# A two-layer decoder trunk on one core: the last up-projection chunk of each feed-forward block also by seven products

## The chip, the cores and the metric

One core of a Trainium2 chip. The time is device microseconds of one launch; lower is better. TensorE (PE) multiplies 128x128 tiles, its weight loads (PEld) run beside it; VectorE (DVE), ScalarE (ACT) and GpSimd (POOL) do elementwise work; SyncE (SP) and POOL issue DMAs. Each engine has its own instruction stream and runs it strictly in order; semaphores tie the streams together.

## The reference

`x` is 512 tokens by 1024. There are two layers, each an attention mixer and then a gated feed-forward block, with root-mean-square norms before and after each. The change touches only the feed-forward block, which both layers have:

```
def conv_ffn(xn, w_up, cw, cb, w_down):          # xn 512x1024, w_up 1024x5632, w_down 2816x1024
    a = xn @ w_up
    a = sum(ap[:, j:j + T] * cw[j] for j in range(3)) + cb      # causal, depthwise over tokens
    gate, val = jnp.split(a, 2, axis=-1)
    return (jax.nn.gelu(gate, approximate=True) * val) @ w_down
```

Everything is float32.

## The kernel before

**Three matmuls for one.** A float32 operand is split into a high part, which a cast to the matmul type gives, and a low part, the rest. Each product is `ah*bh + ah*bl + al*bh` (`mm3`, lines 292 to 294), into one PSUM bank. So every weight needs a cast on ACT (high) and a subtraction on DVE (low). In some places the low part is made another way: ACT writes the negative of the raw weight (`scale=-1.0`) rounded to the matmul type, and an adding DMA from POOL's queue adds the raw weight to it in SBUF.

**Chunks.** The up-projection's 2 x 2816 columns are done in 22 chunks `c` of 128 gate and 128 value columns, features on partitions and the 512 tokens in the free dimension. A plain chunk is two banks (gate and value) of 8 steps over the contraction, 3 matmuls each, 512 wide: 48 matmuls. A chunk in `SEVEN` uses Winograd's form of Strassen's algorithm over halves of the tokens and the contraction and the two column groups: seven products of 12 matmuls, 256 wide (84), some of them accumulated onto each other in PSUM. Its operands are sums of the four weight blocks A11, A12, A21, A22 (`S1` to `S4`, made in `seven_weights`), and sums of the inputs (`XA`, `XB`). The four quarters `o1` to `o4` of its two banks are finished with copies on ACT (`s1`, `u2`, `s7`) and three additions on DVE. `open_seven` does the first product of the next chunk ahead of the last product (`S4`) of the current one. Before, chunks 3 to 20 are so done and 0, 1, 2 and 21 are plain.

**After the matmuls** come, for each of the two banks: the middle tap of the convolution with the bias on ACT (`first_tap`), the two other taps on DVE (`other_taps`, two instructions), then the GELU on ACT (`glu`) and the product of gate and value on POOL (`product`), which a DMA stores in DRAM (`hD`).

**Down-projection.** `down` works on 11 pairs `j` of chunks, again with seven products. In its first part `mul_one(j, bp)` does four of them (12 matmuls, 512 wide) for each token block `bp`, in the order (0,0), (1,0), (0,1), (1,1), (2,0), (2,1), (3,0) and so on; pair 0 opens all eight PSUM banks, four for each `bp`. A pair needs three operands, called `wa`, `wb` (weights) and `ac` (activations): two raw weight tiles (loaded by SP; some sums of w_down lie ready in DRAM as `dT`) and the activations `dact` (from `hD`), whose three sums `pair_sums` makes on DVE. `pair_highs` casts the three on ACT, `pair_lows` subtracts on DVE. In `mul_one` the first of the four products uses `wa`, the second and third `wb`, the fourth `wa`; the low part of the weight is read by the second matmul of each product, the low part of `ac` by the third.

**Order.** It is written out by hand (`manual_schedule`): each engine does its instructions in the order in which the program gives them. The loop over `c` has generators (`step`) that put pieces of the next chunks' weight work between the current chunk's. Below, c is the chunk, m = c + 1 and n = c + 2.

Of the kernel before, what the change touches and what calls it, by code (L numbers as in the profile page):

```python
# [108 lines left out]
def trunk_kernel(ctx, tc, x, norm_gains, w_qkv_a, w_o_a, w_q_b, w_o_b, kv_norm, w_kvf, b_f,  # L109
# [581 lines left out]
    def ffn(l, bd, cp, nxt, ahead):  # L691
# [4 lines left out]
        def first_tap(bb, i, ps, ch):  # L696
            act.activation(bb[:, i, :], ps, AF.Identity, bias=cp[:, 3, ch:ch + 1], scale=cp[:, 2, ch:ch + 1])  # L697

        def other_taps(bb, i, ps, ch):
            for n in (1, 2):  # L700
                dve.scalar_tensor_tensor(bb[:, i, n:], ps[:, :T - n], cp[:, 2 - n, ch:ch + 1], bb[:, i, n:],  # L701
                                         ALU.mult, ALU.add)

        def taps(c, banks, between=None):
            bb = t4([128, 2, T], name="bb")
            for i, ch in ((0, c), (1, NF + c)):
                first_tap(bb, i, banks[i], ch)
                other_taps(bb, i, banks[i], ch)
                if i == 0 and between is not None:
                    between()  # L710
            return bb

        gated = []

        def product():

            if gated:
                c, bb = gated.pop()
                hc[c] = t2([128, T], name="hc")
                pool.tensor_tensor(hc[c], bb[:, 0, :], bb[:, 1, :], ALU.mult)  # L720
                if c - 1 in hc:
                    pool.dma_start(hD[c - 1], hc.pop(c - 1))

# [1 line left out]
            act.activation(bb[:, 0, :], bb[:, 0, :], AF.Gelu_apprx_tanh)  # L725
            gated.append((c, bb))

        def post(c, banks, between=None, bb=None):
            product()
            if bb is None:  # L730
                bb = taps(c, banks, between)
            else:
                first_tap(bb, 0, banks[0], c)
                other_taps(bb, 0, banks[0], c)
                if between is not None:
                    between()
            glu(c, bb)

        xT = None
        XA, XB = [], []  # L740
# [51 lines left out]
            yield  # L792
            dve.tensor_tensor(v[:, 1], r0, v[:, 0].bitcast(F32), ALU.subtract)

        def plain_weights(c):
            W.high_added()
            yield
            W.high()
            yield
            W.low()  # L800

        gens = {}

        def step(c, n=1):

            if c >= NF or c < 0:
                return
            if c not in gens:
                gens[c] = (seven_weights if c in SEVEN else plain_weights)(c)
# [5 lines left out]
        a11, s1_, s3_, s2_ = (slice(i * 256, i * 256 + 256) for i in range(4))  # L815

        def pair_load(j):

# [14 lines left out]
        def pair_highs(j):  # L833

            raws[j] = [*W.take(2), acts.pop(j)]
            one[j] = [t8([128, 2, 1024], F32R, name="w") for _ in range(3)]
            for w, r in zip(one[j], raws[j]):
                act.copy(w[:, 0], r)

        def pair_lows(j):  # L840
            parts = [*zip(one[j], raws.pop(j))]
            for w, r in (parts[0], parts[2], parts[1]) if j == 2 else (parts[2], parts[0], parts[1]):
                dve.tensor_tensor(w[:, 1], r, w[:, 0].bitcast(F32), ALU.subtract)  # L843

        def load_two(j):

# [61 lines left out]
            p_11(j, bp)  # L908
            p_12(j, bp)

        def run(steps):
            for _ in steps:
                pass

        def down(nxt, ahead):
            pair_highs(3)
            for bp in range(2):
                for j in range(2):
                    mul_one(j, bp)
            for j in range(1, ND - 2):  # L920
                if j > 1:
                    mul_one(j, 0)
                    mul_one(j, 1)
                if j + 3 < ND:
                    pair_sums(j + 3)
                    pair_lows(j + 2)
                    pair_highs(j + 3)
                elif j + 3 == ND:
                    pair_lows(j + 2)
                    load_two(0)  # L930
            pair_two(0)
            pair_two(1)
# [76 lines left out]
        step(S0, 2)  # L1009
        post(0, first[0:2])  # L1010
        step(S0, 2)
        begun = opened = half_taps = None
        kept = []
        beside = sums_beside(kept, (l, ND - 1), (1, 8 + l))
        before = 1, first[2:4]
# [11 lines left out]
        for c in range(2, NF):  # L1027
            if c == NF - 4:
                pair_load(0)
            m, n = c + 1, c + 2  # L1030
            if c in SEVEN:
                x21, x22 = [(xT[0][i], xT[1][i], s) for i, s in ((1, LO), (1, HI))]
                banks, s1 = opened
                opened = None
                w = halves.pop(c)
                W.n_get += 2
                o1, o2, o3, o4 = banks[0][:, LO], banks[0][:, HI], banks[1][:, LO], banks[1][:, HI]
                u2, s7 = (t2([128, 256], name="csum") for _ in range(2))
# [3 lines left out]
                bb = half_taps or t4([128, 2, T], name="bb")  # L1042
                cb, prev = before
                for i, ch in ((1, NF + cb), (0, cb)):
                    if i == 0 or half_taps is None:
                        first_tap(bb, i, prev[i], ch)
                        other_taps(bb, i, prev[i], ch)
                half_taps = None
                if n in SEVEN:
                    step(n)  # L1050
                act.copy(u2, o2)
                step(n, 1 if n in SEVEN else 2)
# [4 lines left out]
                if m in SEVEN:  # L1057
                    step(m, 2)
                if n in SEVEN:
                    step(n)  # L1060
                next(beside, None)
                dve.tensor_tensor(o1, o1, s1, ALU.add)
                if m in SEVEN:
                    step(m)
                prod(o3, w.pop("A22"), (*XB, LO))
                dve.tensor_tensor(o4, o2, s7, ALU.add)
                dve.tensor_tensor(o3, o3, u2, ALU.add)
                if n in SEVEN:
                    step(n)
                half_taps = t4([128, 2, T], name="bb")  # L1070
                first_tap(half_taps, 1, banks[1], NF + c)
                if m in SEVEN:
                    opened = open_seven(m)
                    step(m)
                else:
                    begun = W.get(), bank([128, T], name="up")
                    up(*begun, range(4))
                    XA.clear()
                    XB.clear()
                    step(m)  # L1080
                    pair_highs(0)
                    pair_sums(1)
                other_taps(half_taps, 1, banks[1], NF + c)
                while kept:
                    sp.dma_start(*kept.pop())
                prod(o2, w.pop("S4"), x22)
            else:
                banks = [bank([128, T], name="up") for _ in range(2)]
                for s in range(2):
                    if s == 0 and begun:  # L1090
                        w, banks[0] = begun
                        up(*begun, range(4, KD))
                        begun = None
                    else:
                        up(W.get(), banks[1 - s if m in SEVEN else s], range(KD))
                    if s == 0 and m in SEVEN:
                        opened = open_seven(m)
                    if s == 0:
                        post(*before, (lambda: pair_lows(0)) if c == NF - 1 else None, half_taps)
                        half_taps = None  # L1100
                        if c == NF - 1:
                            pair_highs(1)
                    if n not in SEVEN:
                        step(n, 2 - s)
                    if s == 0 and m in SEVEN:
                        half_taps = t4([128, 2, T], name="bb")
                        first_tap(half_taps, 1, banks[1], NF + c)
                        other_taps(half_taps, 1, banks[1], NF + c)
            before = c, banks
            if c == NF - 3:  # L1110
                pair_sums(0)
# [916 lines left out]
```

## Time and profile before

| | us |
|---|---|
| median of 3 runs (1091.5 to 1092.33) | 1092.04 |
| the profiled execution, its own time | 1092.08 |
| span in its profile, first to last instruction | 1090.3 |
| PE busy | 1081.9 (99%) |
| DVE / ACT / POOL busy | 908.7 / 750.9 / 304.5 |
| first feed-forward block: first matmul of chunk 20 after its opening product | 385.64 |
| first feed-forward block: first matmul of the down-projection | 405.21 |
| the same two in the second block | 959.78, 979.35 |

The profile's page lists busy time by engine, the span in 40 slices, DMA queues, the chain of work that ended last, and the costliest groups. In the timeline a row is a start, a duration, the engine, the line, what is written and read, and in brackets the idle time before it with what ended that. PE's rows overlap, since matmuls are pipelined: what a matmul costs is the distance from one start to the next.

### The profile page before, as it was taken

The numbers are of one execution on the slowest core, as the hardware profiler recorded it, in microseconds if no ns is written. First come the engines' busy times: TensorE is split into PE (matmuls) and PEld (weight loads), VectorE is DVE, ScalarE is ACT, GpSimd is POOL, SyncE is SP. The second block draws the span as 40 slices with busy tenths as digits, with TensorE's granted clock in tenths as the row PEclk, the third lists the DMA queues.
The fourth block names the chain that finished last, engine by engine and source line by source line (L and its number), as shares of the span: only waits on it lengthen the run. The fifth ranks groups of instructions, "written<-read, shape, count | busy, mean of one in ns | idle before, by whom it ended". The sixth has DMA issues, their size and how long they took to land.

```text
span 1090.3 us, 20004 instructions
## 1 busy us (share of the span) xinstructions
PE 1081.9 (99%) x7184; PEld 964.7 (88%) x7184; DVE 908.7 (83%) x1510; ACT 750.9 (69%) x1290; POOL 304.5 (28%) x405
## 2 busy tenths in 40 slices
PE   9999999999999999999999999999999999999997
PEld 6988889999999998888888788789999999998886
DVE  6677768898999889997877877937898998989995
ACT  6654587778788757576565677766787878756573
POOL 4632110333333322000010667610233333322000
PEclk9999999999999999999999999999999999999999
DMA  9679895689999978894872776597689999978972
GB/s 314 137 275 407 339 238 156 145 204 233 248 227 223 258 230 319 326 319 106 213 155 78 215 228 196 159 291 185 131 206 240 241 226 239 239 228 315 343 261 77
DMA packets 198251, 250.03 MB, mean 229 GB/s; under 512 B 13888, under 2 KB 141880, under 8 KB 197640
## 3 DMA queue, kind: packets, MB, share of 16 engines
q1 hardware_dynamic: 175976, 181.86, 52.0%
q0 software_dynamic: 22176, 66.90, 28.5%
q8 instruction: 56, 0.92, 0.3%
q14 instruction: 43, 0.35, 0.1%
HBM read 170.28 MB, written 39.63 MB: 193 GB/s over the span
## 4 chain that ended last, share of the span: by engine, by line
PE 91%; DVE 4%; ACT 2%; issue 1%; DMA 0%; SPq 0%; DVEq 0%; ACTq 0%
PE up L292 12%; PE up L293 12%; PE up L294 12%; PE acc L293 7%; PE acc L292 7%; PE acc L294 7%; DVE w L843 2%; PE v_ps L292 2%; PE v_ps L293 2%; PE v_ps L294 2%; PE qk_ps L1361 2%; PE o_ps L1880 2%; PE s_ps L1833 2%; PE q_ps L292 2%; PE pT_ps L1865 2%; PE first L294 1%
## 5 line engine op out<-in xcount | busy, mean ns | idle before, releaser
L292 PE MATMUL up<-xsh,w 128*128 128x256 f32 x576 | 163.1, 283 | 0.0
L293 PE MATMUL up<-xsl,w 128*128 128x256 f32 x576 | 163.0, 283 | 0.0
L294 PE MATMUL up<-xsh,w 128*128 128x256 f32 x576 | 163.0, 283 | 0.0
L701 DVE SCALAR_TENSOR_TENSOR bb<-up,conv,bb 128x511 f32<-128x511 f32 (+1 forms) x160 | 119.4, 747 | 11.7 <-ACT bb L697 8.9
L292 PE MATMUL acc<-w 128*128 128x512 f32 (+1 forms) x311 | 120.6, 388 | 0.0
L294 PE MATMUL acc<-w 128*128 128x512 f32 (+1 forms) x311 | 120.4, 387 | 0.0
L293 PEld LDWEIGHTS up<-xsl,w 128*128 128x128 f32 x576 | 110.6, 192 | 0.1
L292 PEld LDWEIGHTS up<-xsh,w 128*128 128x128 f32 x576 | 110.6, 192 | 0.1
L294 PEld LDWEIGHTS up<-xsh,w 128*128 128x128 f32 x576 | 110.6, 192 | 0.0
L293 PE MATMUL acc<-w 128*128 128x512 f32 (+1 forms) x267 | 103.5, 388 | 0.1
L697 ACT ACTIVATE bb<-up,conv 128x512 f32<-128x512 f32 x80 | 62.3, 779 | 44.3 <-PE up L294 34.2
L770 POOL DMA_DIRECT2D w<-wraw x36 | 30.8, 857 | 164.2 <-ACT w L769 146.5
L720 POOL TENSOR_TENSOR hc<-bb 128x512 f32<-128x512 f32 x44 | 68.4, 1555 | 22.8 <-ACT bb L725 14.5
L60 ACT CAST w<-wraw 128x1024 fp32r<-128x1024 f32 x64 | 66.5, 1051 | 8.1 <-issue 3.8
L294 PEld LDWEIGHTS acc<-w 128*128 128x128 f32 x311 | 58.4, 188 | 11.9
L292 PEld LDWEIGHTS acc<-w 128*128 128x128 f32 x311 | 58.4, 188 | 11.9
L69 DVE TENSOR_TENSOR w<-wraw,w 128x1024 fp32r<-128x1024 f32 x44 | 54.3, 1249 | 10.6 <-ACT w L60 10.5
L293 PEld LDWEIGHTS acc<-w 128*128 128x128 f32 x267 | 50.1, 188 | 11.0 <-DVE w L843 0.9
L781 ACT CAST w<-wsum 128x1024 fp32r<-128x1024 f32 x36 | 37.9, 1052 | 30.2 <-DVE wsum L778 30.2
L843 DVE TENSOR_TENSOR w<-wraw,w 128x1024 fp32r<-128x1024 f32 x44 | 54.1, 1266 | 0.0
L293 PE MATMUL up<-xbl,w 128*128 128x256 f32 (+1 forms) x176 | 53.2, 303 | 0.0
L293 PE MATMUL up<-xcl,w 128*128 128x256 f32 (+1 forms) x176 | 53.2, 303 | 0.0
(348 smaller groups left out, 3482.3 us busy)
## 6 DMA issues: line engine op xcount, KB each, us to landing
wraw<-in_w_up_dram SPq DMA_DIRECT2D x144, 256.0 KB
w<-wraw POOLq DMA_DIRECT2D x56, 512.0 KB, 6.3
dT<-dsums SPq DMA_DIRECT2D x34, 512.0 KB
hD<-hc POOLq DMA_DIRECT2D x44, 256.0 KB, 6.2
dact<-hD SPq DMA_DIRECT2D x44, 256.0 KB
wraw<-dT SPq DMA_DIRECT2D x22, 512.0 KB
wraw<-in_w_down_dram SPq DMA_DIRECT2D x22, 512.0 KB
dsums<-in_w_down_dram SPq DMA_DIRECT2D x36, 256.0 KB
```

What stands on the lines that cost most here:

```text
L60: self.nc.scalar.copy(pair[:, 0, s], raw[:, s])
L69: self.nc.vector.tensor_tensor(pair[:, 1, s], raw[:, s], pair[:, 0, s].bitcast(F32), ALU.subtract)
L292: pe.matmul(o, ah, bh, start=first, stop=False, skip_group_check=shared)
L293: pe.matmul(o, ah, bl, start=False, stop=False, skip_group_check=shared)
L294: pe.matmul(o, al, bh, start=False, stop=last, skip_group_check=shared)
L697: act.activation(bb[:, i, :], ps, AF.Identity, bias=cp[:, 3, ch:ch + 1], scale=cp[:, 2, ch:ch + 1])
L701: dve.scalar_tensor_tensor(bb[:, i, n:], ps[:, :T - n], cp[:, 2 - n, ch:ch + 1], bb[:, i, n:], ALU.mult, ALU.add)
L720: pool.tensor_tensor(hc[c], bb[:, 0, :], bb[:, 1, :], ALU.mult)
L770: pool.dma_start(b[:, 1], r1, accum_op=ALU.add)
L781: act.copy(u[:, 0], sb)
L843: dve.tensor_tensor(w[:, 1], r, w[:, 0].bitcast(F32), ALU.subtract)
L1361: pe.matmul(o, ax(0, b, kc)[x], w[:, k, :], start=kc == 0 and x == 0 and w is wh, stop=kc == KD - 1 and w is wl)
```

## The change

`SEVEN` goes from chunks 3..20 to chunks 3..21, so chunk 21 is done by seven products too, in each of the two feed-forward blocks. The plain way for chunk 21 (`plain_weights`, `begun`, the branches on `n in SEVEN`) goes away. Chunk 21 gets a tail of its own, with the first weight work of the down-projection between its products:

```
@@ SEVEN
-SEVEN = tuple(range(3, 21))
+SEVEN = tuple(range(3, 22))
@@ pair_highs, and a new function behind it
-            for w, r in zip(one[j], raws[j]):
+            parts = [*zip(one[j], raws[j])]
+            for w, r in (parts[2], parts[0], parts[1]) if j < 2 else parts:
                 act.copy(w[:, 0], r)
+                if j == 0:
+                    yield
+
+        def pair_third():
+            j = 2
+            raw = W.take(2)
+            one[j] = wa, wb, ac = [t8([128, 2, 1024], F32R, name="w") for _ in range(3)]
+            act.copy(wa[:, 0], raw[0])
+            act.copy(wb[:, 0], raw[1])
+            act.activation(wb[:, 1], raw[1], AF.Copy, scale=-1.0)
+            pool.dma_start(wb[:, 1], raw[1], accum_op=ALU.add)
+            yield
+            pair_sums(j)
+            k = acts.pop(j)
+            act.copy(ac[:, 0], k)
+            for w, r in ((wa, raw[0]), (ac, k)):
+                dve.tensor_tensor(w[:, 1], r, w[:, 0].bitcast(F32), ALU.subtract)
@@ the loop over chunks, behind the first two products of chunk c (o2 by S2, o3 by S3)
+                if m == NF:
+                    u5 = t2([128, 256], name="csum")
+                    act.copy(u2, o2)
+                    prod(o1, w.pop("A12"), x21)
+                    highs = pair_highs(0)
+                    next(highs)
+                    act.copy(s7, o3)
+                    next(highs)
+                    prod(o2, w.pop("S1"), (*XA, LO))
+                    run(highs)
+                    act.copy(u5, o2)
+                    prod(o3, w.pop("A22"), (*XB, LO))
+                    glu(cb, bb)
+                    run(pair_lows(0))
+                    run(pair_highs(1))
+                    prod(o2, w.pop("S4"), x22)
+                    dve.tensor_tensor(o3, o3, u2, ALU.add)
+                    dve.tensor_tensor(o4, u5, s7, ALU.add)
+                    run(pair_lows(1))
+                    dve.tensor_tensor(o1, o1, s1, ALU.add)
+                    half_taps = t4([128, 2, T], name="bb")
+                    for i in (1, 0):
+                        first_tap(half_taps, i, banks[i], i * NF + c)
+                    for i in (1, 0):
+                        other_taps(half_taps, i, banks[i], i * NF + c)
+                    third = pair_third()
+                    next(third)
+                    product()
+                    glu(c, half_taps)
+                    run(third)
+                    break
...
+                if c >= NF - 3:
+                    pair_sums(c - NF + 3)
...
@@ behind the loop
-        pair_lows(1)
-        post(*before)
-        pair_sums(2)
-        pair_highs(2)
-        pair_lows(2)
         pair_sums(3)
-        product()
+        product(dve)
         pool.dma_start(hD[NF - 1], hc.pop(NF - 1))
```

So `o4` is formed from two copies in SBUF (`u5` and `s7`) instead of from PSUM and a copy; the sums of pairs 0 and 1 come in chunks 19 and 20; of pair 2's three low parts DVE makes two and the adding DMA one (`wb`); and the last chunk's gate product is on DVE instead of POOL. For pair 3 the lows come in the order wa, wb, ac, where they were ac, wa, wb. The rest of the diff puts `plain_weights` and the branches for a plain chunk 21 out of the loop.

How the rows move on ACT, from chunk 20's value tap on. Before (L697 is a first tap, L725 the GELU, L838 a cast of `pair_highs`; the row L697 with x2 is chunk 21's two taps, what stands ahead of it is of chunk 20):

```order
L697 ACTIVATE bb<-up,conv 128x512
L838 CAST w<-wraw 128x1024 x2
L838 CAST w<-dact 128x1024
L697 ACTIVATE bb<-up,conv 128x512
L725 ACTIVATE bb<-bb 128x512
L838 CAST w<-wraw 128x1024 x2
L838 CAST w<-dact 128x1024
L697 ACTIVATE bb<-up,conv 128x512 x2
L725 ACTIVATE bb<-bb 128x512
L838 CAST w<-wraw 128x1024 x2
L838 CAST w<-dact 128x1024
```

After, from the `u2` copy of chunk 21 on (L1055, L1059, L1063 are u2, s7, u5; L827 `pair_highs` of pairs 0 and 1; L697 x2 the first taps of chunk 21; L835 to L837 `pair_third`):

```order
L1055 COPY csum<-up 128x256
L827 CAST w<-dact 128x1024
L1059 COPY csum<-up 128x256
L827 CAST w<-wraw 128x1024 x2
L1063 COPY csum<-up 128x256
L723 ACTIVATE bb<-bb 128x512
L827 CAST w<-dact 128x1024
L827 CAST w<-wraw 128x1024 x2
L697 ACTIVATE bb<-up,conv 128x512 x2
L835 CAST w<-wraw 128x1024
L836 CAST w<-wraw 128x1024
L837 ACTIVATE w<-wraw 128x1024
```

All six casts of pairs 0 and 1 stand ahead of chunk 21's first taps in both; new among them are the three copies. Pair 2's two weight casts and the new negative stand behind them and ahead of its GELU (which follows L837).

On DVE, after, from the lows of pair 0 to the third pair (L849 lows; L1069, L1070, L1072 the additions of o3, o4, o1; L701 other taps of chunk 21; L816 to L818 `pair_sums`; L844 the third pair's two lows; rows of equal text are merged):

```order
L849 TENSOR_TENSOR w<-dact,w 128x1024
L849 TENSOR_TENSOR w<-wraw,w 128x1024 x2
L1069 TENSOR_TENSOR up<-up,csum 128x256
L1070 TENSOR_TENSOR up<-csum 128x256
L849 TENSOR_TENSOR w<-dact,w 128x1024
L849 TENSOR_TENSOR w<-wraw,w 128x1024 x2
L1072 TENSOR_TENSOR up<-up,csum 128x256
L701 SCALAR_TENSOR_TENSOR bb<-up,conv,bb 128x511
L701 SCALAR_TENSOR_TENSOR bb<-up,conv,bb 128x510
```

The addition of o1, for which chunk 21's gate tap on ACT waits, stands behind six lows. In before the six lows of pairs 0 and 1 stood there too, but no additions with them, since chunk 21 was plain.

On POOL, after, the rows from pair 1's sums on (L838 is the adding DMA, L718 a gate product, L720 its store, L819 the store of a sum of activations):

```order
L819 DMA sD<-dact 128x256
L718 TENSOR_TENSOR hc<-bb 128x512
L720 DMA hD<-hc 128x512
L838 DMA w<-wraw 128x1024
L718 TENSOR_TENSOR hc<-bb 128x512
L720 DMA hD<-hc 128x512
L819 DMA sD<-dact 128x256 x2
```

The adding DMA is new there. Behind it on POOL stand chunk 20's gate product and the stores.

More of the change, by code (lines that the diff above doesn't have):

```diff
@@ L702, in other_taps, with taps @@
                                          ALU.mult, ALU.add)
-        def taps(c, banks, between=None):
+        def taps(c, banks):
             bb = t4([128, 2, T], name="bb")
@@ L708, in taps, with product @@
                 other_taps(bb, i, banks[i], ch)
-                if i == 0 and between is not None:
-                    between()
             return bb
         gated = []
-        def product():
+        def product(eng=pool):
             if gated:
@@ L726, in glu, with post @@
             gated.append((c, bb))
-        def post(c, banks, between=None, bb=None):
+        def post(c, banks):
             product()
[L730 to L737, printed above, removed]
+            glu(c, taps(c, banks))
         xT = None
@@ L815, in ffn, with run @@
         a11, s1_, s3_, s2_ = (slice(i * 256, i * 256 + 256) for i in range(4))
+        def run(steps):
+            for _ in steps:
+                pass
         def pair_load(j):
@@ L909, in p_1 @@
             p_12(j, bp)
-        def run(steps):
-            for _ in steps:
-                pass
         def down(nxt, ahead):
-            pair_highs(3)
+            run(pair_highs(3))
             for bp in range(2):
@@ L1011, in ffn @@
         step(S0, 2)
[L1012 removed]
+        opened = half_taps = None
         kept = []
@@ L1067, in ffn @@
                 dve.tensor_tensor(o3, o3, u2, ALU.add)
-                if n in SEVEN:
-                    step(n)
+                step(n)
                 half_taps = t4([128, 2, T], name="bb")
                 first_tap(half_taps, 1, banks[1], NF + c)
[L1072 to L1082, printed above, removed]
+                opened = open_seven(m)
+                step(m)
+                if c >= NF - 3:
+                    pair_sums(c - NF + 3)
                 other_taps(half_taps, 1, banks[1], NF + c)
@@ L1088, in ffn @@
                 banks = [bank([128, T], name="up") for _ in range(2)]
[L1089 to L1108, printed above, removed]
-            before = c, banks
-            if c == NF - 3:
-                pair_sums(0)
-        pair_lows(1)
-        post(*before)
-        pair_sums(2)
-        pair_highs(2)
-        pair_lows(2)
+                up(W.get(), banks[1], range(KD))
+                opened = open_seven(m)
+                post(*before)
+                half_taps = t4([128, 2, T], name="bb")
+                first_tap(half_taps, 1, banks[1], NF + c)
+                other_taps(half_taps, 1, banks[1], NF + c)
+                up(W.get(), banks[0], range(KD))
+            before = c, banks
         pair_sums(3)
-        product()
+        product(dve)
         pool.dma_start(hD[NF - 1], hc.pop(NF - 1))
```

48 lines of the change are left out of this document (20 added, 28 removed).

## The prediction

> **What bounds the kernel now.** I read the page's first, second and fourth part, then the stages by windows, then the timeline of each engine around the end of the chunks.
>
> ```profile
> span 1090.3 us, 20004 instructions
> PE 1081.9 (99%) x7184; PEld 964.7 (88%) x7184; DVE 908.7 (83%) x1510; ACT 750.9 (69%) x1290; POOL 304.5 (28%) x405
> PEclk9999999999999999999999999999999999999999
> PE 91%; DVE 4%; ACT 2%; issue 1%; DMA 0%; SPq 0%; DVEq 0%; ACTq 0%
> ```
>
> PE is busy 99% of the span, holds 91% of the chain that ended last, and its clock is full in every slice. So the end moves by what PE has to do and by what PE must newly wait for, and by nothing else. Three stages (start and end, length, then busy time by engine):
>
> ```profile
> 375.54:385.64 10.10, 10.10 (x86) 10.10 (x85) 8.67 (x13) 7.72 (x11) 2.17 (x3) 1.00 0.84 208
> 385.64:405.21 19.57, 19.57 (x122) 17.66 (x121) 15.45 (x22) 10.49 (x14) 6.75 (x8) 1.00 0.73 235
> 959.78:979.35 19.57, 19.57 (x123) 17.65 (x122) 15.45 (x22) 10.48 (x14) 6.74 (x8) 1.00 0.73 233
> ```
>
> The first is a whole chunk by seven products: 10.10 us. The second is what the change rebuilds: the rest of chunk 20, then chunk 21 done plainly, up to the first matmul of the down-projection. The third is the same in the second block, with the same length, so all below is worked out for the first block and taken twice. PE's rows there:
>
> ```profile
> 385.64 0.28 PE L292 MATMUL up<-xsh,w 128*128 128x256 f32 x1
> 405.21 0.39 PE L292 MATMUL acc<-w 128*128 128x512 f32 x1
> 416.09 0.39 PE L292 MATMUL acc<-w 128*128 128x512 f32 x1
> 422.21 0.39 PE L292 MATMUL acc<-w 128*128 128x512 f32 x1
> 422.65 0.50 PE L293 MATMUL acc<-w 128*128 128x512 f32 x1
> 422.99 0.40 PE L294 MATMUL acc<-w 128*128 128x512 f32 x1
> ```
>
> From 405.21 to 416.09 are 48 matmuls (pairs 0 and 1): 0.227 us from start to start. A 256-wide one takes 10.10/84 = 0.120. The last three rows are the one place near it where PE lost time: steps of 0.44 and 0.34 for 0.227, together 0.32 us, at pair 3's second product.
>
> **PE's work.** With seven products the stretch is one chunk period plus the six products left of chunk 21: 10.08 + 72 x 0.120 = 18.72 us for 19.57 (10.08 being 84 x 0.120): 0.85 less in each block. Chunk 21 then starts at 395.72, the down-projection at 404.36, pair 2 at 404.36 + 10.88 = 415.24. That is all the change can save by itself: 1.7 us, or 0.16%.
>
> **Chunk 21's weights and chunk 20.** These get the DVE work of any such chunk. DVE's steps:
>
> ```profile
> 378.00 0.68 DVE L777 TENSOR_TENSOR wraw<-wraw 128x512 f32<-128x512 f32 x1
> 378.77 1.22 DVE L778 TENSOR_TENSOR wsum<-wraw 128x1024 f32<-128x1024 f32 x1
> 380.03 0.69 DVE L783 TENSOR_TENSOR wraw<-wraw,wsum 128x512 f32<-128x512 f32 x1
> 382.16 1.23 DVE L790 TENSOR_TENSOR w<-wsum,w 128x1024 fp32r<-128x1024 f32 x1 [0.23 <-ACT w L781]
> 383.31 0.42 DVE L1066 TENSOR_TENSOR up<-up,csum 128x256 f32<-128x256 f32 x1
> 384.11 1.21 DVE L793 TENSOR_TENSOR w<-wraw,w 128x1024 fp32r<-128x1024 f32 x1
> 385.24 1.53 DVE L701 SCALAR_TENSOR_TENSOR bb<-up,conv,bb 128x511 f32<-128x511 f32 x2
> 386.68 0.42 DVE L828 TENSOR_TENSOR dact<-dact 128x256 f32<-128x256 f32 x1
> 387.94 1.53 DVE L701 SCALAR_TENSOR_TENSOR bb<-up,conv,bb 128x511 f32<-128x511 f32 x2
> 399.87 1.22 DVE L843 TENSOR_TENSOR w<-dact,w 128x1024 fp32r<-128x1024 f32 x1
> 401.00 3.45 DVE L843 TENSOR_TENSOR w<-wraw,w 128x1024 fp32r<-128x1024 f32 x2
> 417.56 1.63 DVE L830 TENSOR_TENSOR dact<-dact 128x256 f32<-128x256 f32 x1
> 420.25 2.35 DVE L843 TENSOR_TENSOR w<-wraw,w 128x1024 fp32r<-128x1024 f32 x2
> ```
>
> Start to start, a low part takes 1.13, the three sums of a pair 1.26, two taps about 1.44. Chunk 19's taps keep their place and end at 387.94 + 1.44 = 389.38. Then in chunk 20 come L777 (0.77), L778 (1.26), L783 and the addition of o1 (to 392.45), the low part L790 (it waits for ACT's cast of the sum, to 393.6), the additions of o4 and o3 (0.80 together, from L1066 to L793), the other low part (1.13), pair 1's sums (1.26) and chunk 20's taps (2.88): DVE is free at 399.70. On the way PE needs two things. S4 of chunk 20, due at 394.28, waits until the addition of o4 has read its bank, at 394.06. Chunk 21's S2, due at 395.72, waits for the copy s1, which stands behind a first tap and ends at 395.60. The margins are 0.2 and 0.1 us: I take nothing for them, and 0.2 us at most.
>
> **From there to pair 2.** DVE goes on without a gap: lows of pair 0 (3 x 1.13, to 403.09), additions of o3 and o4 (0.8; A22 is ready at 403.1), lows of pair 1 (3.39, to 407.3), addition of o1, finished at 407.73. Pair 1's last low is needed at 404.36 + 2.72 + 0.9 = 407.98: in time by 0.6. The two banks that chunk 21 holds are freed by its taps at 409.1 and 410.5, and the third and fourth product of (0,1) want them at 411.2 and 411.9: in time. ACT and POOL:
>
> ```profile
> 378.39 1.06 ACT L62 ACTIVATE w<-wraw 128x1024 fp32r<-128x1024 f32 x1
> 384.91 0.36 ACT L1024 COPY csum<-up 128x256 f32<-128x256 f32 x1
> 402.47 1.05 ACT L838 CAST w<-dact 128x1024 fp32r<-128x1024 f32 x1
> 403.42 0.78 ACT L697 ACTIVATE bb<-up,conv 128x512 f32<-128x512 f32 x1
> 379.76 0.87 POOL L86 DMA_DIRECT2D w<-wraw  x1 [2.91 <-ACT w L62]
> 400.77 1.47 POOL L720 TENSOR_TENSOR hc<-bb 128x512 f32<-128x512 f32 x1 [1.72 <-ACT bb L725]
> ```
>
> A cast or a negative is 1.05, or 0.95 from start to start; a first tap 0.78 or, by the same tenth, some 0.7 from start to start; the adding DMA's issue starts 0.3 after ACT's negative ends (378.39 + 1.06 to 379.76). The new copies u5 and the order of ACT's six casts cost nothing, since ACT is through with them at 405.4 and then waits. Its last tap of chunk 21 needs o1, added at 407.73. So: tap 407.76, cast wa 408.45, cast wb 409.40, negative 410.35 to 411.41, POOL issues the adding DMA at 411.71. Nothing stands ahead of it on POOL by then. PE reads that low part with the fifth matmul of pair 2, at 415.24 + 4 x 0.227 = 416.15. So the DMA has 4.44 us to land.
>
> **The adding DMA.** It is the one price that no row gives at its new place, but the same DMA of the same 512 KB runs 56 times. The tile's view and, for three issues, the DMA view (SP's traffic in MB while it was under way, and its time to landing):
>
> ```profile
> DMA to landing us min/median/max: 4.5/6.3/10.1
> q1 hardware_dynamic: 54, 0.16, 8.4%
> w<-wraw POOLq DMA_DIRECT2D x1, 512.0 KB, 4.6
> q1 hardware_dynamic: 187, 0.54, 28.3%
> w<-wraw POOLq DMA_DIRECT2D x1, 512.0 KB, 5.5
> q1 hardware_dynamic: 1482, 0.74, 43.8%
> w<-wraw POOLq DMA_DIRECT2D x1, 512.0 KB, 6.0
> w<-wraw POOLq DMA_DIRECT2D x1, 512.0 KB, 7.4
> ```
>
> These are the issues at 653.94, 640.88, 354.00 and, for the last row, 374.16, beside which SP loaded a whole megabyte. Landing follows what SP moves. In the new place SP is quiet at the issue, but its queue holds a 512 KB weight load that waits for a buffer, freed by pair 2's first low on DVE (o1 407.73, taps to 410.5, sums to 411.8, low to 413.0), and then 384 KB of activations and another weight tile from about 414.7. I count 0.5 to 0.75 MB in its flight and take 5.9 us, between the second and third of these. The bounds are 4.5 and 7.4. So PE stalls 5.9 - 4.44 = 1.46 us, between 0.06 and 2.96.
>
> The Trainium skill's page "DMA: Bandwidth & Descriptors", section "Anatomy of one DMA — SWDGE (gpsimd) path", puts such a DMA at about 2.0 us plus bytes over 436 GB/s, by which I estimate 3.2 us: no stall at all, and 2.3 us gained in the sum below. No landing of this form in the trace is under 4.5, so the rows decide.
>
> **What else moves.** The stall of 0.32 at pair 3 came from DVE: L830 took 1.63 for 0.42 beside a gate product on POOL, and pair 3's low ended at 422.60. Now chunk 20's product follows the adding DMA on POOL (412.6 to 413.9) and holds up pair 2's low of `ac` to 415.1 at worst, needed at 415.7. Then sums 1.26, the last product (now DVE's, 0.7), and pair 3's lows at 418.2, 419.4 and 420.5, needed from 420.9 on: that stall goes. Late next would be pair 4's lows: the last ends at 426.4 and is needed at 427.0 even without a stall ahead of it. So I take nothing for them.
>
> **Sum.** Per block -0.85 - 0.32 + 1.46 = +0.29, for two blocks +0.6 us. Against the profiled execution's own 1092.08 (span 1090.3 and 1.8 around it; 0.04 above the median) that is 1092.7, 1092.6 against the median. I say 1092.6. A difference of 0.2%, 2.2 us, is about what a measurement of this kernel can tell from no change.
>
> **Rivals.**
> - *The DMA is hidden.* It lands in 4.5 to 5.0 us as in the quiet issue at 653.94, if SP's load comes late. Stall 0.06 to 0.56, the sum -2.2 to -1.2: about 1090.4. For it: SP is idle when it is issued. Against: the load it competes with is released 1.3 us later. The skill's formula above would end here, with 1089.7.
> - *The DMA comes late* (slower). Above a landing of 6.7 us the stall passes 2.26, and the kernel is slower by more than 0.2%; with the 7.4 of the issue at 374.16 the stall is 2.96, the sum +3.6: 1095.6. For it: three of SP's transfers wait to start in its flight. Against: together they are under the megabyte of that issue, and start later.
> - *Chunk 20 holds up chunk 21.* If one DVE step more than I count (1.13) falls ahead of the additions in chunk 20, S4 waits 0.9; the adding DMA then slips by 1.13 and PE by 0.9, so its stall grows by 0.2. Per block 0.29 + 0.9 + 0.2 = 1.4, in all 1094.8. Against: the same DVE steps ran in chunk 19 of the trace with no PE wait.
> - *The issue is held by DVE.* If POOL can't write descriptors while DVE works from two SBUF inputs, the DMA starts only at 414.1: landing 2.4 later, 0.29 + 2.4 per block, 1097.4. Against: the issue at 379.76 took 0.87 beside DVE's L778 and L783. The Trainium skill, "SBUF — State Buffer", "Who interferes with whom", says GpSimd is locked out by DVE's two-port modes; it infers that such two-input operations leave descriptor writing alone, and the row agrees.
>
> **Chances.** Forecast (stall 0.6 to 2.2) 0.56; hidden 0.22, of which 0.08 lies beyond 0.2%; late DMA 0.15; chunk 20 late 0.05; held issue 0.02. So faster 0.08, slower 0.15 + 0.05 + 0.02 = 0.22, same 0.70. The forecast's own range is 1091.0 to 1094.2; for 8 in 10 I go to 1090.2, inside the hidden case, and to 1095.2, nearly to the late one.
>
> **What would show it.** Right: the down-projection starts 18.7 us after chunk 20's S2; the fifth matmul of pair 2 starts 1 to 2 us late, waiting for the adding DMA; no stall at pair 3. Wrong: that stall is missing or over 2.2; PE waits inside chunks 20 or 21; the adding DMA issued later than 16.0 us after chunk 21's S2; or a new wait in pairs 4 to 10.

## The result, and the profile after

The changed kernel takes 1102.53 us, the median of 6 runs (1099.19 to 1104.34), and the kernel before on the same chip 1092.01 (6 runs, 1091.5 to 1092.33). The ratio is 1.0091, with a 95% interval of [1.0073, 1.0108]. It is slower, by 10.5 us, where 0.6 was forecast. The profiled execution of after took 1102.85 (span 1101.1), against 1092.08 (span 1090.3) for that of before, so the two traces differ by 10.8 us, much as the runs do.

The page of after, the lines that answer to those of before (busy time, the clock over 40 slices, the chain that ended last):

```profile
PE 1084.9 (99%) x7256; PEld 969.5 (88%) x7256; DVE 914.4 (83%) x1524; ACT 758.5 (69%) x1306; POOL 305.1 (28%) x407
PEclk9999999999999998999999999999999999999999
PE 87%; DMA 4%; issue 3%; DVE 3%; ACT 2%; POOL 0%; SPq 0%; DVEq 0%; POOLq 0%; ACTq 0%
```

Two things are new. DMA has 4% of the chain where it had 0%, and the clock has an 8 in the sixteenth slice (413 to 440 us), where before had 9 in each. PE's busy time rose by 3 us although its work shrank, because a matmul at half clock counts as busy for longer: "PE 99%" looks the same and says nothing here. PE's waits of after name the DMA:

```profile
PE acc L293 <- DMA w<-wraw: 7.1, 2, 4.0
```

Two waits, 7.1 us in all, the longest 4.0: one in each block. Before had no wait of PE for a DMA in either place. PE's timeline of after, around pair 2 of the first block and of the second (start, duration, operation, idle time before it):

```profile
404.54 0.40 PE L292 MATMUL acc<-w 128*128 128x512 f32 x1
...
416.12 0.39 PE L292 MATMUL acc<-w 128*128 128x512 f32 x1
420.53 0.80 PE L293 MATMUL acc<-w 128*128 128x512 f32 x1 [4.01 <-DMA w<-wraw]
421.12 0.63 PE L294 MATMUL acc<-w 128*128 128x512 f32 x1
421.55 0.63 PE L292 MATMUL acc<-w 128*128 128x512 f32 x1
...
426.67 0.39 PE L292 MATMUL acc<-w 128*128 128x512 f32 x1
...
997.00 0.39 PE L292 MATMUL acc<-w 128*128 128x512 f32 x1
1000.50 0.80 PE L293 MATMUL acc<-w 128*128 128x512 f32 x1 [3.11 <-DMA w<-wraw]
...
1094.97 0.28 PE L294 MATMUL acc<-w 128*128 128x256 f32 x1
```

The matmul that uses the adding DMA's tile starts at 420.53 and not at 416.12 + 0.227 = 416.35: a stall of 4.18 us, and 3.27 in the second block. Behind it the matmuls follow one another by 0.43 us (421.12 to 421.55) until 426.67, from where it is 0.23 again. Windows of after say why (start and end, length, busy time by engine with counts, granted clock, DMA share, GB/s):

```profile
416.50:420.60 4.10, 0.09 (x2) 0.07 (x1) 4.10 (x5) 2.94 (x3) 1.62 (x3) 0.91 1.03 312
420.60:426.40 5.80, 5.80 (x14) 4.54 (x15) 5.66 (x10) 3.89 (x4) 1.08 (x2) 0.50 1.03 402
426.40:432.00 5.60, 5.60 (x26) 4.57 (x25) 5.50 (x9) 3.01 (x3) 0.54 (x1) 0.98 1.05 400
405.00:440.00 35.00, 30.98 (x124) 25.02 (x123) 34.45 (x47) 22.62 (x25) 7.89 (x12) 0.90 0.97 351
1000.10:1003.50 3.40, 3.00 (x7) 2.43 (x8) 3.30 (x7) 1.08 (x2) 0.30 (x1) 0.50 1.04 405
```

The window from 405 to 440 of before:

```profile
405.00:440.00 35.00, 34.95 (x154) 28.62 (x153) 34.45 (x45) 23.39 (x24) 6.15 (x10) 1.00 0.92 330
```

In the 5.8 us after the stall the granted clock is 0.50, and PE does 14 matmuls where the next 5.6 us hold 26. The last row is the second block's: 0.50 there too, for 3.4 us. The Trainium skill's page "TensorE: Matmul & The Clock Gate", section "Part 1: The HAM clock gate (the "warmup" mystery)", says that PE's clock halves after an idle window of about 3.4 us, and that this window runs freely. Of the two stalls of this trace the first, 4.0 us, is longer than that and the second, 3.1 us, a little shorter; both were followed by the half clock, and experiment 6 below shows it after less.

From 405 to 440 PE does 124 matmuls, 30 fewer than before: 30 x 0.227 = 6.8 us. The sum over the traces: each block starts its down-projection about 0.85 us earlier by the smaller PE work (-1.7), the old stalls of 0.32 are gone (-0.6), the new stalls cost 4.18 + 3.27 = 7.45, the half clock 3.0 in the first block and 1.5 in the second (what its steps, from 420.53 to 426.67 and from 1000.50 to 1003.59, take beyond 0.227 each). That makes 9.6. Between the blocks, from 512 to 584 us, PE is 71.48 us busy where it was 71.87, and the lateness grows by 0.9, of which 0.1 is made up later. PE's waits of after have two entries for it, which those of before do not have:

```profile
PE v_ps L292 <- DVE v_ps L1741: 0.2, 1, 0.2
PE v_ps L293 <- DVE w L1658: 0.2, 1, 0.2
```

They are at 575.83 and 579.26, in the second layer's attention mixer: steps of 0.59 and 0.57 for 0.227, each with one of 0.34 behind it. With 0.8 for this and 0.2 at the start of the span the sum is 10.6 for the 10.5 us by which the last matmul starts later (1094.97 for 1084.44). Why DVE comes late there stays open.

Why the landing took so long shows on the queues. The timeline of after, two rows of SP's queue and the issue of the adding DMA on POOL:

```profile
409.92 0.61 SPq L51 DMA_DIRECT2D wraw<-in_w_down_dram  x1
410.57 3.05 SPq L51 DMA_DIRECT2D wraw<-dT  x2
411.97 0.88 POOL L838 DMA_DIRECT2D w<-wraw  x1 [12.56 <-ACT w L837]
```

The DMA view of after from 411.7 to 420.5 (of SP's queue q1 the packets, MB and share; then the issues of that stretch, KB each, and us to landing where it falls inside):

```profile
q1 hardware_dynamic: 956, 2.08, 63.4%
...
w<-wraw POOLq DMA_DIRECT2D x1, 512.0 KB, 8.5
wraw<-dT SPq DMA_DIRECT2D x1, 512.0 KB
dact<-hD SPq DMA_DIRECT2D x1, 256.0 KB, 8.4
...
wraw<-in_w_down_dram SPq DMA_DIRECT2D x1, 256.0 KB
wraw<-dT SPq DMA_DIRECT2D x1, 256.0 KB
dact<-hD SPq DMA_DIRECT2D x1, 128.0 KB
```

The adding DMA was issued at 411.97 and took 8.5 us (7.6 in the second block). In that time SP's queue moved 2.08 MB. What SP issued in it adds up to 1.4 MB, not all of which had landed by the end; so at least 0.6 MB was already under way, among it the loads of 409.92 and 410.57 (the second DMA of that row, of 512 KB, is issued only at 413.30). SP was not quiet there.

### The profile page after: what moved, and what is told of

Same layout as the page of the kernel before. It is cut to its first block, busy times and chain, and to the rows that moved or that the text cites. A ratio compares the mean times of both kernels' runs of the same rounds, so it can differ in the third digit from the quotient of the medians.

```text
span 1101.1 us, 20223 instructions
## 1 busy us (share of the span) xinstructions
PE 1084.9 (99%) x7256; PEld 969.5 (88%) x7256; DVE 914.4 (83%) x1524; ACT 758.5 (69%) x1306; POOL 305.1 (28%) x407
## 4 chain that ended last, share of the span: by engine, by line
PE 87%; DMA 4%; issue 3%; DVE 3%; ACT 2%; POOL 0%; SPq 0%; DVEq 0%; POOLq 0%; ACTq 0%
PE up L293 12%; PE up L292 12%; PE up L294 12%; PE acc L293 8%; PE acc L294 8%; PE acc L292 8%; PE qk_ps L1364 2%; PE o_ps L1883 2%; PE s_ps L1836 2%; PE q_ps L292 2%; PE pT_ps L1868 2%; DMA w<-wraw 1%; PE first L294 1%; PE first L292 1%; PE first L293 1%
## 5 line engine op out<-in xcount | busy, mean ns | idle before, releaser
L294 PE MATMUL up<-xsh,w 128*128 128x256 f32 x608 | 172.1, 283 | 0.0
L293 PE MATMUL up<-xsl,w 128*128 128x256 f32 x608 | 172.1, 283 | 0.0
L292 PE MATMUL up<-xsh,w 128*128 128x256 f32 x608 | 172.1, 283 | 0.0
L701 DVE SCALAR_TENSOR_TENSOR bb<-up,conv,bb 128x511 f32<-128x511 f32 (+1 forms) x160 | 119.1, 747 | 10.5 <-ACT bb L697 7.7
L294 PE MATMUL acc<-w 128*128 128x512 f32 (+1 forms) x311 | 122.0, 392 | 0.0
L292 PE MATMUL acc<-w 128*128 128x512 f32 (+1 forms) x311 | 122.0, 392 | 0.0
L292 PEld LDWEIGHTS up<-xsh,w 128*128 128x128 f32 x608 | 116.7, 192 | 0.1
L293 PEld LDWEIGHTS up<-xsl,w 128*128 128x128 f32 x608 | 116.7, 192 | 0.1
L294 PEld LDWEIGHTS up<-xsh,w 128*128 128x128 f32 x608 | 116.7, 192 | 0.0
L293 PE MATMUL acc<-w 128*128 128x512 f32 (+1 forms) x267 | 105.4, 395 | 7.1 <-DMA w<-wraw 7.1
L697 ACT ACTIVATE bb<-up,conv 128x512 f32<-128x512 f32 x80 | 62.3, 779 | 40.1 <-PE up L294 33.6
L718 POOL TENSOR_TENSOR hc<-bb 128x512 f32<-128x512 f32 x42 | 66.4, 1581 | 19.3 <-ACT bb L723 11.0
L294 PEld LDWEIGHTS acc<-w 128*128 128x128 f32 x311 | 59.5, 191 | 12.2
L292 PEld LDWEIGHTS acc<-w 128*128 128x128 f32 x311 | 59.4, 191 | 12.2
L60 ACT CAST w<-wraw 128x1024 fp32r<-128x1024 f32 x60 | 62.3, 1051 | 7.5 <-issue 3.9
L293 PEld LDWEIGHTS acc<-w 128*128 128x128 f32 x267 | 51.2, 192 | 18.5 <-DMA w<-wraw 8.0
L69 DVE TENSOR_TENSOR w<-wraw,w 128x1024 fp32r<-128x1024 f32 x42 | 51.7, 1245 | 9.7 <-ACT w L60 9.5
L827 ACT CAST w<-wraw 128x1024 fp32r<-128x1024 f32 x40 | 40.0, 1048 | 15.6 <-PE acc L294 10.7
L755 POOL DMA_DIRECT2D wa<-wraw x38 | 32.6, 858 | 63.0 <-ACT wa L754 59.6
L292 PE MATMUL up<-xbh,w 128*128 128x256 f32 (+1 forms) x168 | 49.3, 293 | 0.0
```

Of the source, the lines that this page charges most:

```text
L60: self.nc.scalar.copy(pair[:, 0, s], raw[:, s])
L69: self.nc.vector.tensor_tensor(pair[:, 1, s], raw[:, s], pair[:, 0, s].bitcast(F32), ALU.subtract)
L292: pe.matmul(o, ah, bh, start=first, stop=False, skip_group_check=shared)
L293: pe.matmul(o, ah, bl, start=False, stop=False, skip_group_check=shared)
L294: pe.matmul(o, al, bh, start=False, stop=last, skip_group_check=shared)
L718: eng.tensor_tensor(hc[c], bb[:, 0, :], bb[:, 1, :], ALU.mult)
```

## The experiments

The main theory: the loss is the adding DMA's landing, which SP's transfers in its flight set, and the half clock that follows PE's stall. The rivals: chunk 21's new form costs the time and the DMA only shows it; DVE's two-input work holds POOL or the port and so delays the DMA; the DMA is long wherever it is issued. The kernels were made from after, if not said otherwise. The kernel before, run with them, took 1092.10 (20 runs) beside experiments 1 to 4 and 1091.88 (19 runs) beside 5 to 8.

**1. The third pair's low by DVE, no adding DMA.** The rest of the change stays.

```
# pair_third
-            act.activation(wb[:, 1], raw[1], AF.Copy, scale=-1.0)
-            pool.dma_start(wb[:, 1], raw[1], accum_op=ALU.add)
...
-            for w, r in ((wa, raw[0]), (ac, k)):
+            for w, r in ((wa, raw[0]), (ac, k), (wb, raw[1])):
```

> The changed kernel, but pair 2's third low part by DVE (behind its other two lows) and no adding DMA and no negative for it. Theory A (the whole loss is the wait for the adding DMA and the half clock behind it): no wait for a DMA at pair 2, full clock there, at most 1 us of waiting for DVE's lows, so 1090.5 to 1092.5 us. Rival B (the longer tail of seven products holds up ACT and DVE, and the DMA only shows it): PE still waits 2 us or more at pair 2 or behind it, over 1096 us.

Measured: 1090.88 us (10 runs, 1089.9 to 1091.24), ratio 0.9987 [0.9978, 0.9996]. It is the fastest of all versions. Windows of this kernel, around pairs 2 to 10 of both blocks:

```profile
405.00:440.00 35.00, 35.00 (x155) 28.91 (x155) 34.45 (x47) 23.58 (x25) 4.86 (x9) 1.00 0.96 327
985.00:1005.00 20.00, 20.00 (x90) 16.51 (x89) 19.69 (x28) 14.50 (x15) 3.76 (x7) 1.00 0.92 322
```

PE is never idle there and the clock is full. So the loss at pair 2 and behind it hangs on the adding DMA, and the seven products for chunk 21 are a small gain: the medians differ by 1.2 us, the profiled spans by 2.0 (1090.3 to 1088.3), where the terms of the prediction without its DMA stall give 2 x (0.85 + 0.32) = 2.3. Of the 2.0 some 0.45 lies ahead of chunk 20, since the down-projection starts 1.32 earlier than before (403.89 for 405.21) and not 0.85. About 0.6 is lost again from 530 to 584 us, most of it in the second layer's mixer, where PE waits for DVE as in after (at 571.27, a step of 0.57 for 0.227). Six of the seven kernels made from after have this wait, and neither kernel with a plain chunk 21 (before, experiment 5) has it: it goes with the new form rather than with the DMA.

**2. SP's loads from pair 4 on wait for the adding DMA.** A tiny store on SP that reads the tile stands ahead of pair 3's sums.

```
+        gD = tc.dram_tile([1, 16], F32, name="gD")
...
+        sp.dma_start(gD, one[2][1][0:1, 1, 0:16].bitcast(F32))
         pair_sums(3)
```

> The changed kernel, but SP's loads of pair 4 and later stand behind a 64-byte store that reads the low part which the adding DMA makes, so they are issued only when it has landed. Theory A1 (it lands late because SP's transfers share the DMA engines): landing 5 to 6 us instead of 7.6 and 8.5, PE waits 1 to 2 us, no half clock, 1091.5 to 1094 us if pair 4's later loads cost nothing. Rival C (DVE, working from two SBUF inputs, keeps POOL from writing the descriptors): landing stays near 8 us, 1100 us or more.

Measured: 1102.0 us (4 runs, 1101.14 to 1103.8), ratio 1.0092 [1.0077, 1.0107]. The DMA view of this kernel, the two adding DMAs:

```profile
w<-wraw POOLq DMA_DIRECT2D x1, 512.0 KB, 4.6
...
w<-wraw POOLq DMA_DIRECT2D x1, 512.0 KB, 5.1
```

Landing fell from 8.5 and 7.6 to 4.6 and 5.1, at the same place on POOL and beside the same DVE work. In the flight of both SP's queue moved nothing. So SP's transfers made the difference, which goes against the port. The time did not fall, as PE's waits of this kernel show:

```profile
PE acc L293 <- DVE w L850: 4.0, 3, 1.9
PE acc L292 <- ACT w L828: 2.1, 2, 1.1
PE acc L293 <- DMA w<-wraw: 0.6, 1, 0.6
```

The wait at pair 2 is 0.6 at most. In its place PE waits two pairs later for ACT's cast and DVE's low of pair 4, whose loads were held back; the half clock follows there too (430.9 to 434.0, granted clock 0.95 as the mean of 405 to 440). The loads have no slack to give.

**3. The adding DMA 3.5 us earlier.** The cast and the negative of `wb` stand between chunk 21's two first taps.

```
# pair_third: wb's part now comes first
-            act.copy(wa[:, 0], raw[0])
             act.copy(wb[:, 0], raw[1])
...
+            yield
+            act.copy(wa[:, 0], raw[0])
             yield
# chunk 21
-                    for i in (1, 0):
-                        first_tap(half_taps, i, banks[i], i * NF + c)
+                    third = pair_third()
+                    first_tap(half_taps, 1, banks[1], NF + c)
+                    next(third)
+                    first_tap(half_taps, 0, banks[0], c)
```

> The changed kernel, but the cast and the negative of pair 2's second weight and its adding DMA stand between the two first taps of chunk 21 on ACT, where ACT waited 1.8 us. Theory A: issue some 3.5 us earlier (about 408.4 in the first block), landing in 6 to 8.5 us as before, so PE waits 0 to 1 us, full clock, 1089.8 to 1092 us. Rival D (it lands when SP's backlog is through, whenever it is issued, near 420): the wait stays 3 us or more and the time over 1098.

Measured: 1092.35 us (10 runs, 1091.89 to 1096.05), ratio 1.0006 [0.9997, 1.0015]: just above what was expected. The adding DMAs, issued at 407.9 and 982.2, in the DMA view of this kernel, with SP's traffic in the flight of the first:

```profile
q1 hardware_dynamic: 1151, 2.07, 66.2%
w<-wraw POOLq DMA_DIRECT2D x1, 512.0 KB, 8.5
...
w<-wraw POOLq DMA_DIRECT2D x1, 512.0 KB, 9.1
```

They land no sooner after the issue (8.5 and 9.1 us, the first beside 2.07 MB), but the issue stands 3.5 us earlier in the block (3.9 us behind the start of the down-projection, where it was 7.4), and so much more of it is hidden. What is left are PE's waits:

```profile
PE acc L293 <- DMA w<-wraw: 1.7, 2, 1.1
```

And its window, with full clock and one matmul fewer than before:

```profile
405.00:440.00 35.00, 34.45 (x153) 28.18 (x152) 34.38 (x49) 24.55 (x26) 7.58 (x12) 1.00 1.01 353
```

The stalls, 0.83 and 1.42 us over two steps each on the timeline, take back what the seven products bring. The earlier issue cures 10.2 of the 10.5 us.

**4. PE kept busy in part of the stall.** 32 bf16 matmuls by a tile of zeros stand ahead of the product that waits; they add zero.

```
+                if (j, bp) == (2, 0) and key == (bp, 1):
+                    for _ in range(32):
+                        pe.matmul(db[bp, 0][:, 0:128], zz, zz, start=False, stop=False, skip_group_check=True)
```

> The changed kernel, and 32 small matmuls of zeros (bf16, 128x128), added onto an open bank, ahead of pair 2's second product in each block: they do nothing but keep PE busy in part of the stall. Theory A2 (an idle time of over 3 us makes the clock fall to half for some us): the wait for the DMA shrinks by what they take, 2 to 3 us, the DMA lands as late as before, the clock stays full, and the 3.0 and 1.5 us of slow matmuls go: about 1098. Rival E (the slow matmuls have another cause, such as weight loads held up by transfers): they stay, 1102 or more.

Measured: 1096.4 us (5 runs, 1095.62 to 1097.18), ratio 1.0036 [1.0022, 1.005]. PE's timeline of this kernel:

```profile
415.59 1.96 PE L897 MATMUL acc<-zz 128*128 128x128 bf16 x32
417.36 0.48 PE L294 MATMUL acc<-w 128*128 128x512 f32 x1
418.38 0.50 PE L295 MATMUL acc<-w 128*128 128x512 f32 x1 [0.54 <-DMA w<-wraw]
```

Its window:

```profile
405.00:440.00 35.00, 34.46 (x176) 28.44 (x175) 34.45 (x46) 25.40 (x28) 7.87 (x12) 1.00 1.01 356
```

With 1.8 us of idling filled by useless work the clock stays full, and 6.1 of the 10.5 us are gone. The half clock (4.5 us) accounts for the larger part; the first block's DMA also landed 1.6 us sooner (6.9), which was not intended and not expected. So the 6.1 is no clean price of the clock. In the second block, where the landing was 7.6 as in after, the clock is full too (1.00 from 985 to 1005), so it is the filled idle time that keeps it, and not the sooner landing.

**5. The adding DMA alone, from before.** Chunk 21 stays plain; pair 2's second low is made by ACT's negative and an adding DMA.

```
# before, pair_highs and pair_lows
+                if (i, j) == (1, 2):
+                    act.activation(w[:, 1], r, AF.Copy, scale=-1.0)
+                    pool.dma_start(w[:, 1], r, accum_op=ALU.add)
...
-            for w, r in (parts[0], parts[2], parts[1]) if j == 2 else (parts[2], parts[0], parts[1]):
+            for w, r in (parts[0], parts[2]) if j == 2 else (parts[2], parts[0], parts[1]):
```

> The kernel before (chunk 21 plain), with one part of the change alone: pair 2's wb gets its low part by ACT's negative and the adding DMA, DVE makes the other two. Theory A: ACT's negative ends near 416 in the first block and PE wants the low part at 417.0, so with a landing of 4.6 to 8.5 us PE waits 4 to 8 us, then half clock, in each block: 1102 to 1114 us. Rival B (the DMA hurts only beside the new tail of chunk 21): 1092 to 1094.

Measured: 1099.76 us (4 runs, 1096.12 to 1103.93), ratio 1.0074 [1.0047, 1.0101]. PE's waits of this kernel:

```profile
PE acc L293 <- DMA w<-wraw: 5.8, 2, 3.1
```

The DMA view, the flight of the first one (issued at 413.6):

```profile
q1 hardware_dynamic: 482, 1.05, 42.6%
w<-wraw POOLq DMA_DIRECT2D x1, 512.0 KB, 7.0
```

Most of the loss, 7.9 us, comes without any change to chunk 21, which puts an end to that rival. It was smaller than expected, since the issue came 2.5 us earlier than I had worked out. The first stall, 3.24 us as a step, was followed by 3.4 us of half clock (421.2 to 424.6), the second, 2.86, by none.

**6. Experiments 2 and 3 together**: earlier issue, and SP's loads behind the adding DMA.

> e3 and e2 together: the adding DMA issued between chunk 21's first taps, and SP's loads from pair 4 on held until it has landed. Theory A1 (SP's transfers under way set the landing, and in e2 it was pair 4's loads that then came late): landing 4.6 to 5.1 us, near 413 in the first block; pair 4's loads start 4 us earlier than in e2, whose two waits together were 3.4 us; so no wait of PE over 0.2 us, 1089.8 to 1091.5, as e1. Rival F (holding the loads costs as such, or DVE's lows are late at pair 4 whatever is loaded): waits at pair 4 stay, over 1094.

Measured: 1097.19 us (4 runs, 1095.69 to 1098.64), ratio 1.0049 [1.0034, 1.0064]: a miss. Landing was 4.6 and 4.6, and PE waits for the adding DMA nowhere. SP and then DVE of this kernel, first block:

```profile
413.58 0.34 SPq L810 DMA_DIRECT2D dact<-hD  x1
...
424.03 0.42 DVE L817 TENSOR_TENSOR dact<-dact 128x256 f32<-128x256 f32 x1 [2.85 <-DMA dact<-hD]
```

SP's first load goes out at 413.58, and DVE stands 2.85 us for those activations, with pair 4's lows behind it. PE's waits:

```profile
PE acc L293 <- DVE w L851: 3.5, 4, 1.8
```

The longest step of PE's timeline was 1.54 us late in the first block and 1.97 in the second, and half clock followed for 3.4 and 3.5 us. I had expected that loads held for 5 us would still come in time.

**7. The last gate product back on POOL**, in the kernel of experiment 1.

```
         pair_sums(3)
-        product(dve)
+        product()
```

> e1 (no adding DMA), but the last chunk's gate product on POOL as before. If the 0.32 us that before lost at pair 3 came from that product (DVE's sums beside it took 1.63 for 0.42), PE waits 0.1 to 0.5 us at pair 3 or 4 in each block, 1091 to 1092 us. Rival (the lows have room now that chunk 20's product runs earlier): no wait, 1090.9 as e1.

Measured: 1091.21 us (10 runs, 1090.36 to 1091.67), ratio 0.9994 [0.9984, 1.0003]. Timeline of this kernel, DVE and then PE:

```profile
416.59 3.46 DVE L847 TENSOR_TENSOR w<-wraw,w 128x1024 fp32r<-128x1024 f32 x2
...
420.72 0.39 PE L293 MATMUL acc<-w 128*128 128x512 f32 x1
421.25 0.50 PE L294 MATMUL acc<-w 128*128 128x512 f32 x1
```

The same two lows in experiment 1, with the product on DVE ahead of them:

```profile
416.94 2.35 DVE L847 TENSOR_TENSOR w<-wraw,w 128x1024 fp32r<-128x1024 f32 x2
```

Beside POOL's product (417.53 to 418.98) the two lows take 3.46 us for 2.35, and PE is late by 0.30 (420.72 to 421.25, less 0.227) and 0.10 in each block: the old stall of pair 3 again, 0.4 us for the 0.32 of the prediction. The medians differ by 0.3 us and the profiled spans by 1.2 (1089.5 for 1088.3), which this stall, 0.8 in both blocks, explains in part.

**8. The fourth quarter from the PSUM banks**, without the copy `u5`, in the kernel of experiment 1.

```
-                    act.copy(u5, o2)
...
+                    dve.tensor_tensor(o4, o2, s7, ALU.add)
                     prod(o2, w.pop("S4"), x22)
...
-                    dve.tensor_tensor(o4, u5, s7, ALU.add)
```

> e1, but chunk 21's fourth quarter from PSUM and s7, as in the other chunks, with no copy u5: S4 then waits until DVE has read the bank, and that stands behind pair 0's three lows. I expect a PE wait of 0.3 to 0.8 us ahead of S4 in each block, 1091.4 to 1092.6 us. Rival (the copy is only off the path): no wait, 1090.9.

Measured: 1091.8 us (10 runs, 1091.21 to 1092.39), ratio 0.9999 [0.9989, 1.0008]. PE's waits of this kernel:

```profile
PE up L292 <- DVE up L1064: 1.1, 2, 0.5
```

S4 must now wait for DVE, 0.68 and 0.10 us as steps in the first block. So the copy keeps 0.8 us a block off PE; the medians differ by 0.9 us, the profiled spans by 1.9 (1090.2 for 1088.3). That it costs nothing, as counted, is borne out by experiment 1, where PE does not wait beside it.

## Why the prediction was wrong

What held, by its own steps:
- PE's work: the down-projection starts at 404.54 (404.36 predicted; the whole trace of after is some 0.2 late from its start). Experiment 1 shows that the gain is real.
- Chunks 20 and 21: no PE wait in either, though the margins were given as 0.2 and 0.1 us.
- The issue: 411.97 for 411.71; of these 0.26 the start of the trace makes the same 0.2. The tile is needed at 416.35, for 416.15. So the time that the DMA had, 4.44 us, came out as 4.38.
- The port: the issue on POOL took 0.88 us beside DVE's lows, and experiment 2 lands in 4.6. "The issue is held by DVE" did not happen.
- Pair 3: the stall went. POOL's product stretched DVE's low as foretold (2.26 us for 1.2). The change also puts pair 4's sums behind pair 3's lows, where they stood ahead of them, which the account of the change leaves out. Experiment 7 keeps that order, and the stall is back with POOL's product; what the order is worth by itself no run shows.

What failed, in order of size:
- **The landing, a term of the sum mis-sized.** Put at 5.9 us with bounds of 4.5 and 7.4, it took 8.5 and 7.6. The rows from which I took it say that landing follows SP's traffic, and the runs agree on the whole: 4.6 and 5.1 with SP's loads held back, 7.0 beside 1.05 MB, 7.6 beside 1.73, 8.5 beside 2.08 (not strictly: 6.6 beside 1.27, 9.1 beside 1.96). The input was wrong. I counted 0.5 to 0.75 MB in the flight, although the loads that I named for it (512 KB, 384 KB and another weight tile of 512 KB) make 1.4 MB. They came when I said (413.30 for 413.0, 414.96 for "about 414.7"), all were issued inside the flight, and at least 0.6 MB of earlier loads was still moving at the issue. I had called SP "quiet at the issue" because it issued nothing just then, which says nothing of what it has under way. The upper bound failed for the same reason: 7.4 us is beside one megabyte, and I ruled out that this place could have more. The row that I quoted, 4.5/6.3/10.1, has landings of up to 10.1 us, and I did not look at what stood beside them. The longest was issued at 731.46 in the trace of before; the queues in its flight (q0 is POOL's, its own 512 KB included):

```profile
q0 software_dynamic: 453, 1.61, 80.1%
q1 hardware_dynamic: 953, 0.48, 17.3%
```

Three more adding DMAs were issued on POOL in the 6 us ahead of it. So what other queues than SP's have under way goes with late landings too. With the stalls measured, 7.45 for 2.92, the term was short by 4.5 us.
- **The half clock, missing from the sum.** A stall of PE was priced at its own length. It cost another 4.5 us. The trace of before could not show it, since its stalls there are 0.2 us; but the rival "late" should have carried it as a condition.
- **A wait outside the two stretches, missing from the sum.** The prediction took every change to lie around chunk 21 and the first pairs. The two waits for DVE in the second layer's mixer cost 0.9 us; why DVE is late there no run shows.

The rival "the DMA comes late" named the right mechanism, at 3.0 us of stall a block and a price of 3.6. Its condition, that of SP's transfers "together they are under the megabyte", is the sentence that was wrong.

## What to carry to other kernels

A DMA's landing is not a property of the DMA: count what every queue has in flight at its issue, buffers that load ahead above all, and take the landing from rows with that much traffic. Where PE would then wait, add the half clock that can follow, or issue the transfer earlier (3.5 us took 10.2 of the 10.5 us away here), or let an engine that has the time to spare (here DVE, 1.1 us) do the work, as in experiment 1. Holding back the other transfers only moved the wait here (experiments 2 and 6), since they were needed soon themselves.

## What the runs showed of the hardware

- PE's idle time has an afterprice: at granted clock 0.50 the 512-wide matmuls started every 0.43 us instead of every 0.227, for 3.1 to 6.1 us after the stall.
- There is no sharp length from which this happens. Single stalls of 0.2 to 1.5 us (before, experiments 3, 4) kept the full clock, and so did one of 2.86 (experiment 5). Half clock came after 3.24, 3.27 and 4.18 us; after 1.2 and 2.2 close to one another (experiment 2); and in experiment 6 with no step late by more than 1.54 and 1.97. The idle window of about 3.4 us that the Trainium skill names on its page "TensorE: Matmul & The Clock Gate" (section "Part 1: The HAM clock gate (the "warmup" mystery)") does not cover those last ones. What decides between 1.5 and 3 us stays open, and so does whether this is why after's runs spread over 5 us and before's over 0.8.
- The same 512 KB adding DMA landed after 4.6 to 9.1 us at nearly the same place of the program. With nothing moving on SP's queue it took 4.6 and 5.1 us (experiment 2), beside 1.05 to 2.08 MB there 6.6 to 9.1.
